# A hybrid decoder block on one core: the recurrence's inverse norm by Newton steps on GpSimd, and pooled tiles loaded into the ring of raw weights

## The chip, the core and the metric

The kernel runs on one core of a Trainium2 chip. The metric is the device time of one execution in microseconds (us). The shapes are fixed: one sequence of 1024 tokens, 1024 channels, 8 heads of 128, four pooling groups of 256 channels, a hidden layer of 4096, everything float32.

The engines are named as in the profile: PE is TensorE's matmul side and PEld its weight load, DVE is VectorE, ACT is ScalarE, POOL is GpSimd, SP is the engine that issues most of the DMAs (SPq is its queue). Each engine takes its instructions in one fixed order.

## What is computed

The reference, cut to what the change touches:

```python
proj = x @ w_in                       # q | f | i | o_gate | pool_v | gate_a | gate_b
o = hgrn2_chunked(...)                # gated recurrence, per head
o = o * rsqrt(mean(o * o) + 1e-6)     # per token and head, over 128 channels
a = (o * hgrn_norm_g * sigmoid(o_gate)) @ w_a
pooled = causal_multiscale_pool(pool_v)           # 4 groups, windows 2, 4, 8, 16
b = concat(pooled[g] @ w_pool[g] for g) * pool_scale
mix = (sigmoid(gate_a) * a + sigmoid(gate_b) * b) @ w_out
x = layer_norm(ALPHA * x + mix)
x = layer_norm(ALPHA * x + relu(x @ w_up) ** 2 @ w_down)
```

## The kernel before, in words

**Products.** Each float32 operand is split into a rounded part and a rest: ACT casts the rounded part (L118), DVE subtracts it from the source to get the rest (L119), and each product is then three matmuls (L105 to L107, or L201, L203, L204). The large projections are 2x2 block products with seven instead of eight block multiplications: `pair` prepares the combinations of weight blocks, `run` walks its seven steps. One step of one pair is 12 matmuls of 128x512.

**Rings.** A weight block arrives as two "raw" tiles from a ring of two buffers (`raw_tile`, 4 KB in each partition), and its split parts lie in a ring of ten "w" tiles (`w_tile`, 2 KB in each partition; `row_tile` is another view of one). A buffer of a ring is handed on when its last reader is done. The recurrence has rings of its own, among them og (2 buffers), v (2), q (3) and f (3), each buffer holding a 128x512 tile.

**The recurrence.** `hgrn(h, u, ...)` works on head h and half u of the tokens, 16 times in all. It decays queries and keys on DVE and POOL (the small chunk factors L819 to L838 are POOL's), transposes keys (L870), forms the state (L875, L883), scores (L887, L898, L905) and outputs in PSUM (L915, L918). Then comes the norm: ACT squares four 128x128 blocks and sums each row (L923), takes the root of the 128x4 sums (L924, which needs another activation table than the sigmoids around it), DVE inverts it (L925), ACT scales the four blocks (L928), PE transposes them (L931), DVE multiplies by the gate (L932), and SP stores the head (L933).

**The order of the work.** The heads are interleaved with the projections: `EXTRAS` lists what follows which half. Behind the last half, (7, 1), stand `gates(4)`, `o_sums(2)`, `pool_products(0)`, `gates(5)`, `pool_products(1)`, `gates(6)`, `pool_products(2)`, `pool_products(3)`, `gates(7)`; the last half itself has a higher priority than these, and so has an `o_sums(3)` inside it, which loads the stored heads 3 and 7 (L594) and adds them up (L608 to L611). The framework records the program and then fixes each engine's order by its own estimate of times; so a small edit can move many instructions. After the heads come `a_pair` (products with w_a), the output product, two layer norms and the hidden layer.

**The pooled products.** `pool_products(g)` loads w_pool of the group into a raw tile (L716) and splits it into q and f buffers. For each half u it loads the two pooled tiles "po" (L594 called from L719) and splits them into w tiles, then does 2 x 6 matmuls (L105 to L107), multiplies by gate and scale (L729, or ACT's L727 for the last group), and stores "pb" (L730). In the kernel before, `room()` hands out q, f, og, v in turn, so the two pooled tiles of a half land in an og and a v buffer of the recurrence's rings.

Of the kernel before, what the change touches and what calls it, by code (L numbers as in the profile page):

```python
# [9 lines left out]
F32 = mybir.dt.float32  # L10
F32R = mybir.dt.float32r
U32 = mybir.dt.uint32
AF = mybir.ActivationFunctionType
ALU = mybir.AluOpType

_TC = dict(schedule_with_timeline_sim=True)
P = 128
# [5 lines left out]
HALF = 512  # L23
CH = HALF // P
# [12 lines left out]
LN_EPS = 1e-5  # L37
RMS_EPS = 1e-6
QSCALE = float(P) ** -0.5
PSUM = bass.MemoryType.PSUM  # L40


@with_exitstack
def tile_hybrid_block(
# [19 lines left out]
    V, A, G, PE = nc.vector, nc.scalar, nc.gpsimd, nc.tensor  # L64
# [5 lines left out]
    const = ctx.enter_context(tc.tile_pool(name="const", bufs=1))  # L70
    pp = ctx.enter_context(tc.tile_pool(name="pp", bufs=4, space=PSUM))
    hd = ctx.enter_context(tc.tile_pool(name="hd", bufs=1, space=bass.MemoryType.DRAM))
# [8 lines left out]
    def nm(s):  # L81
        seq[0] += 1
        return f"{s}_{seq[0]}"
# [7 lines left out]
    def ps_tile(tag="pj", bufs=4):  # L91
        if tag == "hg":
            hg_tags.append(hg_tags.pop(0))
            tag, bufs = hg_tags[-1], 1
        return pp.tile([P, HALF], F32, tag=tag, name=nm("ps_" + tag), bufs=bufs)

    def f(t):
        return t.bitcast(F32)
# [17 lines left out]
    def split(src, tile_of):  # L116
        hi, lo = tile_of(), tile_of()
        A.copy(hi, src)  # L118
        V.tensor_sub(lo, src, f(hi))  # L119
        return hi, lo  # L120
# [11 lines left out]
        out=cmask, in_=cmask, compare_op=ALU.is_ge, fill=0.0, base=0,  # L132
        pattern=[[1, P]], channel_multiplier=-1,
    )
    eps_rms = const.tile([P, 1], F32, name="eps_rms")
    G.memset(eps_rms, RMS_EPS)
    eps_ln = const.tile([P, 1], F32, name="eps_ln")
    G.memset(eps_ln, LN_EPS)
    inv_n = const.tile([P, HALO], F32, name="inv_n")
# [66 lines left out]
    def raw_tile():  # L206
        return wq.tile([P, CH, 2, P], F32, tag="raw", name=nm("raw"), bufs=2)
# [20 lines left out]
    def loaded_blocks(*args):  # L228
        raw, load = w_blocks(*args)
        load(0, 1)  # L230
        return raw
# [28 lines left out]
    def c_late():  # L260
        return c_tile(False)
# [133 lines left out]
    def dram(name, width=HALF):  # L395
        return hd.tile([P, width], F32, tag=name, name=name)
# [5 lines left out]
    with tc.tile_pool(name="xr", bufs=8, side="right", reuse_waits="tile") as xr:  # L402
# [17 lines left out]
        V.tensor_sub(e01[:, 8:16], prm[:, 8:16], lb)  # L420
        A.activation(e01, e01, AF.Exp)
        V.tensor_add(lb, e01[:, 0:8], e01[:, 8:16])
# [157 lines left out]
    pod = [[dram(f"po{j}_{u}") for u in range(2)] for j in range(8)]  # L580
# [11 lines left out]
    def loaded(src, tile_of):  # L592
        t = tile_of()
        nc.sync.dma_start(out=t, in_=src)  # L594
        return t
# [22 lines left out]
    with tc.tile_pool(name="tmp", bufs=1, side="right", reuse_waits="tile") as tmp:  # L618
# [14 lines left out]
        def tt(tag, dtype=F32):  # L633
            pool = tmp if tag in ("q", "f", "og", "v") else hgp
            return pool.tile([P, HALF], dtype, tag=tag, name=nm(tag), bufs=RINGS.get(tag, 1))

        def small(tag, shape, bufs=2):
            n = math.prod(shape[1:])
            t = hgp.tile([P, max(n, LINE)], F32, tag=tag, name=nm(tag), bufs=bufs)[:, :n]
            return t if len(shape) == 2 else t.rearrange("p (a b) -> p a b", b=shape[2])  # L640


        def head_inputs(h, behind=()):
# [6 lines left out]
            def take_f(u):  # L650
                def take(src):
                    t = fs[u] = fs[u] or tt("f")
                    A.activation(t, src, AF.Sigmoid)
                    A.activation(t, t, AF.Identity, bias=lb[:, h : h + 1], scale=one_lb[:, h : h + 1])
                return take

            def take_q(u):
                def take(src):
                    t = qs[u] = tt("q")
                    A.activation(t, src, AF.Sigmoid)  # L660
                    V.scalar_tensor_tensor(t, src, QSCALE, t, ALU.mult, ALU.mult)
                return take
# [11 lines left out]
        def output_gates(h):  # L674

            def take(dst, src=False):
                def put(t):
                    s = c_late() if src else t
                    A.activation(s, t, AF.Sigmoid)
                    nc.sync.dma_start(out=dst, in_=s)  # L680
# [7 lines left out]
        def gates(j):  # L688
# [3 lines left out]
            def take(dst, src=None, more=None):  # L692
                def put(t):
                    s = (tt("v") if spare else c_late()) if src else t
                    more_of = loaded(more, lambda: tt("v")) if more is not None else None
                    A.activation(s, t, AF.Sigmoid)
                    if more_of is not None:
# [10 lines left out]
        def pool_products(g):  # L708

            tags = iter(("q", "f", "og", "v") * 3)  # L710

            def room(dtype=F32):
                return tt(next(tags), dtype)

            raw = raw_tile().rearrange("p k n c -> p (k n c)")[:, : 2 * 2 * P].rearrange("p (k c) -> p k c", c=2 * P)
            nc.sync.dma_start(out=raw, in_=w_pool[g].rearrange("(k p) c -> p k c", p=P))  # L716
            wh, wl = split(raw, lambda: room(F32R).rearrange("p (k c) -> p k c", c=2 * P))
            for u in range(2):
                pl = [split(loaded(pod[2 * g + i][u], room), row_tile) for i in range(2)]  # L719
                for i in range(2):  # L720
                    w = slice(i * P, (i + 1) * P)
                    j = 2 * g + i
                    t = room() if j == KT - 1 else loaded(gbd[j][u], room)
                    ps = ps_tile()
                    mm3(ps, [(wh[:, c, w], wl[:, c, w], *pl[c]) for c in range(2)])
                    if j == KT - 1:
                        A.activation(t, ps, AF.Copy, scale=pscale[:, j : j + 1])  # L727
                    else:
                        V.scalar_tensor_tensor(t, ps, pscale[:, j : j + 1], t, ALU.mult, ALU.mult)  # L729
                    nc.sync.dma_start(out=pbd[j][u], in_=t)  # L730

        def pooled(g):

            j, win = 2 * g, WINDOWS[g]

            def mean(c, u):

                for lo in (QUARTER, 0):
                    pv = c[:, lo : lo + HALO + QUARTER]
                    cur = pv  # L740
                    for lev in range(g + 1):
                        s = 1 << lev
                        nx = small("pA" if lev % 2 == 0 else "pC", [P, HALO + QUARTER + HALO], 1)[:, : HALO + QUARTER]
                        V.tensor_add(nx[:, 2 * s - 1 :], cur[:, 2 * s - 1 :], cur[:, s - 1 : HALO + QUARTER - s])
                        cur = nx
                    n = HALO
                    if u == 0 and lo == 0:
                        n += win - 1
                        V.tensor_mul(cur[:, HALO:n], cur[:, HALO:n], inv_n[:, : win - 1])
                        V.tensor_sub(pv[:, HALO:n], cur[:, HALO:n], pv[:, HALO:n])  # L750
                    V.scalar_tensor_tensor(pv[:, n:], cur[:, n:], 1.0 / win, pv[:, n:], ALU.mult, ALU.subtract)

            def put(c, i, u):
                nc.sync.dma_start(out=pod[j + i][u], in_=c[:, HALO:])

            wide = [[None, None], [None, None]]
            before = small("bef", [P, HALO])

            def room(i, u):
                wide[i][u] = c_wide(False)  # L760
                return wide[i][u][:, HALO:]

            def first(c, i):
                G.memset(c[:, :HALO], 0.0)
                mean(c, 0)
                put(c, i, 0)

            def second(c, i):
                mean(c, 1)
                put(c, i, 1)  # L770

            def take_11(_):
                c = wide[0][0]
                A.copy(before, c[:, HALF:])
                first(c, 0)

            def take_21(_):
                c = wide[0][1]
                A.copy(c[:, :HALO], before)
                second(c, 0)  # L780

            def take_12(ps):
                c, c22 = c_wide(True), wide[1][1]
                A.copy(c[:, HALO:], ps)
                A.copy(c22[:, :HALO], c[:, HALF:])
                first(c, 1)
                second(c22, 1)

            run(pair(
                loaded_blocks(w_in, 4 * D + j * P, 4 * D + (j + 1) * P),  # L790
                (lambda: room(0, 0), lambda: room(0, 1), lambda: room(1, 1)), (take_11, take_12, take_21, lambda _: None),
            ))

        def blk(t):
            return t.rearrange("p (b s) -> p b s", s=SUB)
# [10 lines left out]
        def hgrn(h, u, ft, q, v, og, state):  # L806
# [5 lines left out]
            k = ft  # L812
# [84 lines left out]
            for c in range(CH):  # L897
# [7 lines left out]
            V.copy_predicated(  # L905
                at, cmask.bitcast(U32).unsqueeze(1).to_broadcast([P, CH, P]),
                sc.rearrange("p (c t) -> p c t", t=P),
# [11 lines left out]
            ss = small("ss", [P, CH])  # L919
            on = tt("tH")  # L920
            for c in range(CH):
                w = slice(c * P, (c + 1) * P)
                A.activation(on[:, w], o[:, w], AF.Square, accum_out=ss[:, c : c + 1])  # L923
            A.activation(ss, ss, AF.Sqrt, bias=eps_rms, scale=1.0 / P)  # L924
            V.reciprocal(ss, ss)  # L925
            for c in range(CH):
                w = slice(c * P, (c + 1) * P)
                A.activation(on[:, w], o[:, w], AF.Copy, scale=ss[:, c : c + 1])  # L928
# [153 lines left out]
    with tc.tile_pool(name="wo", bufs=1, side="right", reuse_waits="tile") as mp:  # L1082
        st1 = [None] * 8
        g1, b1 = ln_params(lambda: f(act_tile()).rearrange("p a b -> p (a b)"), ln1_g, ln1_b)
        for k2 in range(0, KT, 2):
            raw = raw_rows(w_out, k2, 1)
            for k in range(2):
                n = len(wo)
# [313 lines left out]
```

## Time and profile before

| What | us |
|---|---|
| time, median of 3 runs | 1464.81 (1462.62 to 1467.08) |
| the profiled execution's own time | 1460.19 |
| its span, first to last instruction | 1458.5 |
| PE busy | 1436.4 |
| DVE busy | 1141.6 |
| ACT busy | 758.3 |
| POOL busy | 58.6 |

The profile is one execution. A group's line gives the source line, the engine, the operation, the tiles it writes and reads, the count, the busy time in us and the mean of one in ns; behind the bar stands the idle time of the engine ahead of such instructions. A view by windows gives for each stretch its length, the busy us of PE, PEld, DVE, ACT and POOL with their instructions in brackets, the granted TensorE clock (1.00 is full), the share of the DMA engines and GB/s. A view of waits gives who waited for whom: us in total, times, the longest. A timeline gives start, length, engine, line and, in brackets, the idle time ahead of an instruction. The list of DMA issues gives the size of one transfer and the median time from issue to landing.

### The profile page before, as it was taken

To read this page: it belongs to the slowest core of one execution; us is meant where nothing else is said; L and a number is where in the kernel's file an instruction comes from. 1 tells how busy PE (TensorE), PEld (TensorE's weight loads), DVE (VectorE), ACT (ScalarE), POOL (GpSimd) and SP (SyncE) were. 2 spreads that over 40 slices of the span, in tenths; PEclk is the share of its full clock that TensorE was granted. 3 is DMA by queue.
4 is the path that set the end of the run, shared out by engine and by line. 5 is a ranking of instruction groups with operands and counts; after the bars stand their busy time and mean duration, and the time that the engine had idled before them with its cause. 6 is when DMAs were issued, how large, how long until landed. Compare 5 with 4: busy or idle time off the path is not lost.

```text
span 1458.5 us, 20662 instructions
## 1 busy us (share of the span) xinstructions
PE 1436.4 (98%) x7377; PEld 1187.9 (81%) x7377; DVE 1141.6 (78%) x1838; ACT 758.3 (52%) x1383; POOL 58.6 (4%) x244
## 2 busy tenths in 40 slices
PE   8999999999999998999999999999999999999997
PEld 7888888888888886788888878888888888888886
DVE  5967989899898885768985597666666787777977
ACT  5445565666656655556542376555555443333535
POOL 0001001001000010000002100000000100000000
PEclk9999999999999999999999999999999999999999
DMA  7232233323234447897672225444474874445322
GB/s 253 70 126 87 85 98 101 109 75 114 90 99 138 152 132 249 301 299 241 223 247 99 73 94 195 159 146 144 152 261 149 275 260 150 153 141 163 130 73 116
DMA packets 160615, 226.82 MB, mean 156 GB/s; under 512 B 11232, under 2 KB 84480, under 8 KB 160512
## 3 DMA queue, kind: packets, MB, share of 16 engines
q1 hardware_dynamic: 158576, 218.93, 44.7%
q0 software_dynamic: 1152, 4.19, 0.8%
q10 hardware_dynamic: 784, 2.38, 0.5%
q8 instruction: 58, 0.95, 0.3%
q14 instruction: 45, 0.37, 0.1%
HBM read 154.16 MB, written 71.30 MB: 155 GB/s over the span
## 4 chain that ended last, share of the span: by engine, by line
PE 94%; DVE 3%; DMA 1%; ACT 1%; issue 0%; SPq 0%; DVEq 0%
PE ps_pj L201 16%; PE ps_pj L203 16%; PE ps_pj L204 16%; PE ps_pj L1283 4%; PE ps_pj L1285 4%; PE ps_pj L1284 4%; PE ps_pj L106 3%; PE ps_pj L107 3%; PE ps_pj L105 2%; PE ps_tr L1285 1%; PE ps_tr L1283 1%; PE ps_tr L1284 1%; PE ps_sc L201 1%; PE ps_sc L203 1%; PE ps_sc L204 1%; PE ps_hg L203 1%
## 5 line engine op out<-in xcount | busy, mean ns | idle before, releaser
L201 PE MATMUL ps_pj<-act,w 128*128 128x512 f32 x1068 | 421.6, 395 | 0.4 <-ACT act L123 0.2
L203 PE MATMUL ps_pj<-act,w 128*128 128x512 f32 x1068 | 415.1, 390 | 0.5 <-DVE act L124 0.5
L204 PE MATMUL ps_pj<-act,w 128*128 128x512 f32 x1068 | 414.1, 390 | 0.0
L201 PEld LDWEIGHTS ps_pj<-act,w 128*128 128x128 f32 x1068 | 200.6, 188 | 42.8 <-ACT act L123 0.6
L204 PEld LDWEIGHTS ps_pj<-act,w 128*128 128x128 f32 x1068 | 200.5, 188 | 42.3
L203 PEld LDWEIGHTS ps_pj<-act,w 128*128 128x128 f32 x1068 | 200.6, 188 | 40.6 <-DVE act L124 0.9
L118 ACT CAST w<-t 128x512 fp32r<-128x512 f32 x170 | 104.7, 620 | 105.0 <-PE ps_pj L203 53.8
L118 ACT CAST w<-raw 128x512 fp32r<-128x512 f32 x143 | 88.2, 620 | 117.3 <-PE ps_pj L203 62.5
L119 DVE TENSOR_TENSOR w<-raw,w 128x512 fp32r<-128x512 f32 x143 | 99.8, 702 | 55.2 <-ACT w L118 53.9
L119 DVE TENSOR_TENSOR w<-t,w 128x512 fp32r<-128x512 f32 x170 | 115.9, 685 | 29.6 <-ACT w L118 29.4
L1245 ACT CAST act<-act 128x1024 fp32r<-128x1024 f32 x66 | 66.9, 1050 | 107.9 <-issue 35.0
L1246 DVE TENSOR_TENSOR act<-act,act 128x1024 fp32r<-128x1024 f32 x66 | 79.3, 1220 | 18.5 <-ACT act L1245 15.8
L1285 PE MATMUL ps_pj<-act,act 128*128 128x512 f32 x240 | 92.9, 389 | 0.0
L1284 PE MATMUL ps_pj<-act,act 128*128 128x512 f32 x240 | 92.9, 389 | 0.0
L1283 PE MATMUL ps_pj<-act,act 128*128 128x512 f32 x240 | 92.4, 389 | 0.0
L275 DVE TENSOR_TENSOR c<-c,ps_pj 128x512 f32<-128x512 f32 x95 | 64.5, 681 | 18.0 <-PE ps_pj L204 13.4
L271 ACT COPY c<-ps_pj 128x512 f32<-128x512 f32 x96 | 55.2, 582 | 12.8 <-PE ps_pj L204 12.8
L817 DVE RECIPROCAL tC<-tA 128x128 f32<-128x128 f32 x64 | 54.1, 904 | 0.0
L1284 PEld LDWEIGHTS ps_pj<-act,act 128*128 128x128 f32 x240 | 45.1, 188 | 9.4
L1285 PEld LDWEIGHTS ps_pj<-act,act 128*128 128x128 f32 x240 | 45.1, 188 | 9.4
L1283 PEld LDWEIGHTS ps_pj<-act,act 128*128 128x128 f32 x240 | 45.1, 188 | 9.3
L241 DVE TENSOR_TENSOR t<-raw,raw 128x512 f32<-128x512 f32 x43 | 29.6, 689 | 21.9 <-DMA raw<-in_w_in_dram 19.7
(415 smaller groups left out, 2719.8 us busy)
## 6 DMA issues: line engine op xcount, KB each, us to landing
h<-c SPq DMA_DIRECT2D x106, 256.0 KB, 2.1
act<-h SPq DMA_DIRECT2D x78, 256.0 KB, 2.9
raw<-in_w_in_dram SPq DMA_DIRECT2D x64, 256.0 KB, 3.4
draw<-in_w_down_dram SPq DMA_DIRECT2D x16, 1024.0 KB, 7.8
raw<-in_w_up_dram SPq DMA_DIRECT2D x30, 512.0 KB, 4.2
raw<-in_w_in_dram SPq DMA_DIRECT2D x18, 512.0 KB, 4.0
hf<-h SPq DMA_DIRECT2D x34, 256.0 KB, 2.9
c<-o SPq DMA_DIRECT2D x24, 256.0 KB, 3.4
```

Source lines behind the costliest of these rows:

```text
L118: A.copy(hi, src)
L119: V.tensor_sub(lo, src, f(hi))
L201: PE.matmul(ps, wh[:, k], th, start=first and k == 0, stop=False, skip_group_check=True)
L203: PE.matmul(ps, wh[:, k], tl, start=False, stop=False, skip_group_check=True)
L204: PE.matmul(ps, wl[:, k], th, start=False, stop=k == CH - 1, skip_group_check=True)
L271: A.copy(t, ps)
L275: V.tensor_add(t, t, ps)
L1245: A.copy(hi, src)
L1246: V.tensor_sub(lo, src, f(hi))
L1283: PE.matmul(ps, hh[:, w], wh, start=fresh and n == 0, stop=False, skip_group_check=True)
L1284: PE.matmul(ps, hh[:, w], wl, start=False, stop=False, skip_group_check=True)
L1285: PE.matmul(ps, hl[:, w], wh, start=False, stop=n == M - 1, skip_group_check=True)
```

## The change

Two edits. First, the root and the reciprocal of the norm (L924, L925) are replaced by `inverse_root`: 14 GpSimd instructions on 128x4 tiles, which take the bits of the number as an integer for a first guess and then make three Newton steps. Its result is a tile "ry", which ACT's scaling (L928) reads instead of "ss". The constant `eps_rms` goes.

Second, the two pooled tiles of a half are loaded into the two halves of one raw tile, `both`, instead of into an og and a v buffer. `room` goes on to hand out q, f, og, v in turn to the other uses of it (the split of w_pool, the loaded gates, the results).

```diff
+ROOT_GUESS = float(0x5F3759DF)
+ROOT_STEPS = 3
...
-    eps_rms = const.tile([P, 1], F32, name="eps_rms")
-    G.memset(eps_rms, RMS_EPS)
...
             for u in range(2):
-                pl = [split(loaded(pod[2 * g + i][u], room), row_tile) for i in range(2)]
+                both = raw_tile().rearrange("p k n c -> p (k n c)").rearrange("p (k c) -> p k c", c=HALF)
+                pl = [split(loaded(pod[2 * g + i][u], lambda: both[:, i]), row_tile) for i in range(2)]
...
+        def inverse_root(total):
+
+            x, y, z = (small(tag, [P, CH]) for tag in ("rx", "ry", "rz"))
+            G.tensor_scalar(x, total, 1.0 / P, RMS_EPS, ALU.mult, ALU.add)
+            G.tensor_scalar(y.bitcast(I32), x.bitcast(I32), -0.5, ROOT_GUESS, ALU.mult, ALU.add)
+            for _ in range(ROOT_STEPS):
+                G.tensor_mul(z, y, y)
+                G.tensor_mul(z, z, x)
+                G.tensor_scalar(z, z, -0.5, 1.5, ALU.mult, ALU.add)
+                G.tensor_mul(y, y, z)
+            return y
...
-            A.activation(ss, ss, AF.Sqrt, bias=eps_rms, scale=1.0 / P)
-            V.reciprocal(ss, ss)
+            ss = inverse_root(ss)
```

Line numbers of the kernel after are higher: by 3 up to the constants, by 1 up to `gates` and `pool_products`, by 13 to 14 from `blk` on. The texts below use the numbers of the kernel before for lines that stand in both.

More of the change, by code (lines that the diff above doesn't have):

```diff
@@ L12 @@
 U32 = mybir.dt.uint32
+I32 = mybir.dt.int32
 AF = mybir.ActivationFunctionType
```

## The prediction, as written before the run

> **What bounds the kernel now.** First the page's head, then the chain that ended last, and the view by windows around the place where the slices of PE dip:
>
> ```profile
> span 1458.5 us, 20662 instructions
> PE 1436.4 (98%) x7377; PEld 1187.9 (81%) x7377; DVE 1141.6 (78%) x1838; ACT 758.3 (52%) x1383; POOL 58.6 (4%) x244
> PE 94%; DVE 3%; DMA 1%; ACT 1%; issue 0%; SPq 0%; DVEq 0%
> ```
>
> ```profile
> 145.00:560.00 415.00, 415.00 (x2763) 345.03 (x2763) 374.35 (x734) 250.82 (x562) 29.35 (x172) 1.00 0.36 113
> 575.00:592.00 17.00, 10.32 (x41) 7.54 (x41) 9.19 (x16) 7.69 (x21) 0.00 (x0) 0.80 0.76 254
> 592.00:640.00 48.00, 48.00 (x212) 39.31 (x211) 31.65 (x51) 22.67 (x39) 0.00 (x0) 1.00 0.95 318
> ```
>
> PE is the bound: 1458.5 - 1436.4 = 22.1 us of idle in all. From 145 to 560 us, which holds almost the whole recurrence, PE has no idle time, so nothing that relieves ACT, DVE or POOL there is worth time. One stretch of 17 us holds 17.00 - 10.32 = 6.7 us of the idle time, and its granted clock of 0.80 costs another 17 x 0.20 = 3.4 us. The view of PE's waits and its timeline tell why:
>
> ```profile
> PE ps_pj L105 <- ACT w L118: 4.7, 1, 4.7
> PE ps_hg L915 <- DVE st L883: 1.2, 1, 1.2
> PE ps_pj L106 <- DVE w L119: 0.8, 1, 0.8
> ```
>
> ```profile
> 572.73 0.39 PE L201 MATMUL ps_pj<-act,w 128*128 128x512 f32 x1
> 572.96 0.39 PE L203 MATMUL ps_pj<-act,w 128*128 128x512 f32 x1
> ...
> 582.85 1.22 PE L105 MATMUL ps_pj<-w,q 128*128 128x512 f32 x2 [4.66 <-ACT w L118]
> ...
> 585.99 0.63 PE L107 MATMUL ps_pj<-w,f 128*128 128x512 f32 x1
> 586.41 0.63 PE L105 MATMUL ps_pj<-w,q 128*128 128x512 f32 x1
> ```
>
> A 128x512 matmul starts 0.23 us after the one before; behind the stall of 4.66 us the step is 0.42 us for a while. The three waits (4.7 + 1.2 + 0.8 = 6.7) are the idle time of that stretch. The chain shows what the longest one waited for:
>
> ```profile
> 573.53 2.31 DMA o<-og
> ...
> 576.27 0.38 SPq L699
> ...
> 577.18 4.97 DMA og<-po
> 582.18 0.62 ACT w L118
> ```
>
> The pooled tile of `pool_products(0)` could be loaded only at 577.18, when the og buffers of the last half came free. **So 6.7 + 3.4 = 10.1 us are to be had in this stretch, and hardly more elsewhere.**
>
> **First edit, the root.** It takes away 16 roots with their table loads, and by the built orders 16 loads that brought the sigmoid's table back (35 loads before, 3 after):
>
> ```profile
> L924 ACT ACT_TABLE_LOAD x16 | 20.5, 1283 | 0.3
> L924 ACT ACTIVATE ss<-ss,eps_rms 128x4 f32<-128x4 f32 x16 | 4.8, 298 | 0.2
> L925 DVE RECIPROCAL ss<-ss 128x4 f32<-128x4 f32 x16 | 2.6, 163 | 5.9 <-ACT ss L924 5.8
> ```
>
> That is 41 us of loads and 4.8 us of roots on ACT, 2.6 us of reciprocals and 5.8 us of waiting on DVE. PE has no idle time where they lie: worth 0.
>
> It adds 14 GpSimd instructions per half, each on the result of the one before. Their nearest rows are small operations of the recurrence:
>
> ```profile
> 401.98 0.22 POOL L823 TENSOR_TENSOR p<-T 128x16 f32<-128x16 f32 x1
> 402.27 0.20 POOL L826 TENSOR_TENSOR p<-p 128x8 f32<-128x8 f32 x1
> ```
>
> ```profile
> L826 POOL TENSOR_TENSOR p<-p x16: 203/204/2201, 127.6 to 537.0; 128x8 f32<-128x8 f32 x16
> L819 POOL COPY T<-tA x16: 229/352/1553, 126.6 to 536.0; 128x32 f32<-128x32 f32 x16
> ```
>
> L826 reads what L823 wrote and starts 0.29 us after it, so 14 x 0.29 = 4.1 us. No row shows GpSimd's multiply-and-add with constants, nor its integer view; from 0.20 us (L826's shortest) to 2.2 us (its longest) each, I take 0.29, the step of the nearest pair. In the chain of a half, 1.28 + 0.30 + 0.16 = 1.7 us become 4.1. What covers them is what stands in PE's order between a half's last L918 and its first transpose L931: in the changed program 47 to 60 large matmuls in fourteen halves and 36 with 23 small ones in another, about 10.7 us or more at 0.23 us, but only 33 (7.5 us) in half (7, 0). Needed are the squares, the root and the first scaling:
>
> ```profile
> L923 ACT ACTIVATE tH<-ps_hg 128x128 f32<-128x128 f32 x64 | 16.9, 279 | 9.1 <-PE ps_hg L918 9.1
> L928 ACT ACTIVATE tH<-ps_hg,ss 128x128 f32<-128x128 f32 x64 | 18.2, 366 | 3.7 <-DVE ss L925 3.7
> ```
>
> The four squares take 4 x 0.28 us, so 1.1 + 4.1 + 0.4 = 5.6 us. In (7, 0) two casts (0.6 us each), one of which needs weights of `gates(5)` that load late, stand on ACT between the squares and the scaling: 0 to 1.5 us of stall, **taken as 0.7**. Without the cover each us more per root would cost up to 16 us.
>
> The first of the 14 instructions waits for ACT's sums. Behind it on POOL stand chunk factors of the next half (L819 to L838), for which DVE's products with T wait. About six DVE instructions at 0.6 to 0.9 us stand between the scan and the first of these, against 0.3 us for each root instruction put in between: taken as 0.
>
> **Second edit, the raw ring.** The two pooled tiles are loaded into a raw buffer. In the changed orders `pool_products(0)` stands before the last half's outputs and 24 large matmuls stand between L875 and L915: all three waits of 575 to 592 go, **-10.1 us**. What is late next? The raw ring has only two buffers, X and Y, and now carries a chain: w_pool[g] in X, then the first half's pooled tiles in X, the second half's in Y, then the next `gates` in X and Y. No link can be loaded before the last is split. The prices, from the list of DMA issues between 540 and 640 us and from the groups:
>
> ```profile
> raw<-in_w_in_dram SPq DMA_DIRECT2D x10, 256.0 KB, 5.6
> og<-po SPq DMA_DIRECT2D x8, 256.0 KB, 3.9
> raw<-in_w_pool_dram SPq DMA_DIRECT2D x4, 256.0 KB, 4.1
> tC<-o SPq DMA_DIRECT2D x1, 256.0 KB, 3.7
> ...
> L118 ACT CAST w<-raw 128x512 fp32r<-128x512 f32 x143 | 88.2, 620 | 117.3 <-PE ps_pj L203 62.5 <-DMA raw<-in_w_in_dram 16.7 <-PE ps_sc L203 10.2
> L932 DVE SCALAR_TENSOR_TENSOR og<-ps_tr,prm,og 128x512 f32<-128x512 f32 x16 | 11.9, 745 | 0.2 <-PE ps_tr L931 0.2
> ```
>
> ```profile
> 590.24 0.68 DVE L119 TENSOR_TENSOR w<-og,w 128x512 fp32r<-128x512 f32 x1
> 590.84 0.68 DVE L119 TENSOR_TENSOR w<-v,w 128x512 fp32r<-128x512 f32 x1
> ```
>
> DVE steps of this size start 0.6 us apart. For groups 0 and 1 the links are covered by 8 and 5 us of matmuls. For **group 2** they meet the end of the recurrence. On SP, the load of w_pool[2] stands right behind the load tC of the last head, which waits for that head's store; on DVE, its split stands behind the sums that need tC. From the gated product L932: store 2.3 us (the chain's row), tC 3.7 with 0.4 us of issue on SP, four DVE steps at 0.6 (two sums, a split, w_pool's split) 2.4, load of po 3.9, cast 0.6, and issues 0.2: 13.5 us. L932 itself is late, since a difference of `gates(6)`'s weights stands three places ahead of it on DVE. The last of these weights is issued when a w buffer has come free (23 matmuls, 5.2 us, ahead of the transposes) and a cast and a split (1.4 us with the issue) have used it, and lands 5.6 + 0.4 us later, 2.2 us behind the first transpose; four DVE steps (2.5 us) later L932 is done, at 4.7. PE has its four transposes (0.5 us) and 61 large matmuls (13.9) in between: 4.7 + 13.5 - 14.4 = **3.8 us of stall**. With the shortest loads of these kinds in this stretch (2.9 and 2.6 us) it vanishes; with the longest (8.5 and 7.9) it is 10:
>
> ```profile
> DMA to landing us min/median/max: 2.9/5.3/8.5
> ...
> DMA to landing us min/median/max: 2.7/3.9/7.9
> ...
> DMA to landing us min/median/max: 2.6/3.6/7.2
> ```
>
> (These are the views by tile of raw, og and v.) For **`gates(7)`**, X comes free only with the split of group 3's first tiles, and ACT's order puts the scaling of the last pooled product, which waits for the product's end, ahead of the first cast: at least 0.2 + 0.6 + 0.6 = 1.4 us of stall, and with a load of 5.6 us, issued 4 us before that end, 2.2; **taken as 2.0**, up to 5. Group 3's own load, behind three 512 KB loads of w_a, adds 0.2.
>
> A new stall may also lower the clock. 4.66 us did so and cost 3.4 us, 1.2 us did not; 3.8 lies between, nearer the first, but PE's full pace had been cut by three waits there: 1 in 4, 0.8 us. [...]
>
> **Sum:** -10.1 + 0.7 + 3.8 + 2.0 + 0.2 + 0.8 = -2.6 us against the profiled execution's 1460.19 (its span and 1.7 us around it): 1457.6. The runs shown have a median of 1464.81, 4.6 us above it, so I expect 1462.2, say **1462**.
>
> **Rivals.** (1) *Clean gain.* The loads land near their short end, since the stretch from 577 on no longer bunches them: group 2's stall goes, `gates(7)` keeps 1.4, half (7, 0) 0.5: -8.2 us, 1456.6. For it: PE waits nowhere from 592 to 640 in spite of 318 GB/s. Against it: the ring's links are in sequence. (2) *Late links, slower.* The loads of the chain land at 8 us, behind the 1.5 MB of w_a: stalls of 10 and 4.5 us, with the clock halved after both (6.8) and 0.7 more: 22 - 10.1 = +11.9, 1476.7. It is slower as soon as the new stalls and their slow clock cost over 10.1 us. (3) *The root outgrows its cover, slower.* It decides where the root takes over 10.7 - 1.5 = 9.2 us, 0.66 us for an instruction; at 1.0 us it is 14, and 15 halves stall by 4.8 us, +72, 1537. L819's median of 0.35 and the longest of 2.2 us speak for it, L826's median of 0.20 against it. [...] (4) *The change does nothing:* the tiles are loaded no earlier and the stall stays, 1464.8; the new order of SP speaks against it.
>
> **Chances.** A run can hardly tell less than 0.3% (4.4 us) from no change. Forecast, with most of the gain given back, and rival 4: 0.43, within 0.3%. Rival 1: 0.40, faster. Rivals 2 and 3: 0.11 and 0.06, slower. The range: down to 1453 (all 10.1 us, less 2 us of spread as in the runs shown), up to 1470, where rival 2 has half its price; beyond lie about 0.15. The forecast's own range is 1458 to 1469.
>
> **What would show it.** Right: no wait of L105 for group 0; a wait of PE at the first matmul of group 2, ended by ACT's cast of a raw tile, and one at the first of `gates(7)`; 3 table loads on ACT; root steps of about 0.3 us; PE without idle time in the recurrence. Wrong: PE waits for L931 in many halves (the root is too slow), or no wait at groups 2 and 3 at all (rival 1).

## The result, and the profile after

| What | us |
|---|---|
| time of the changed kernel, median of 4 runs | 1488.41 (1487.62 to 1491.49) |
| time of the kernel before beside it, median of 4 runs | 1464.82 (1462.62 to 1467.08) |
| ratio | 1.0165, 95% interval 1.0144 to 1.0186 |
| the profiled execution's own time, and its span | 1488.09, 1486.4 |

The change makes the kernel 23.6 us slower. The forecast was 1462, its range ended at 1470, and no rival named what happened. The head of the profile's page of the changed kernel, and its chain by engines:

```profile
span 1486.4 us, 20806 instructions
PE 1463.7 (98%) x7377; PEld 1192.3 (80%) x7377; DVE 1142.7 (77%) x1822; ACT 715.2 (48%) x1335; POOL 120.4 (8%) x467
PE 91%; DVE 4%; DMA 3%; issue 1%; ACT 1%; SPq 0%; DVEq 0%; ACTq 0%
```

PE has the same 7377 matmuls, and its idle time is 1486.4 - 1463.7 = 22.7 us, against 22.1 before. So the span did not grow by waits. PE's *busy* time grew, by 1463.7 - 1436.4 = 27.3 us: the matmuls themselves take longer. The view by lines, kept apart by shape, tells which. The kernel before (after the bar's first number, the busy time, stands the mean of one in ns):

```profile
L201 PE MATMUL ps_pj<-act,w 128*128 128x512 f32 x1068 | 421.6, 395 | 0.4 <-ACT act L123 0.2 <-ACT og L271 0.2
L203 PE MATMUL ps_pj<-act,w 128*128 128x512 f32 x1068 | 415.1, 390 | 0.5 <-DVE act L124 0.5
L204 PE MATMUL ps_pj<-act,w 128*128 128x512 f32 x1068 | 414.1, 390 | 0.0
L1285 PE MATMUL ps_pj<-act,act 128*128 128x512 f32 x240 | 92.9, 389 | 0.0
```

The changed kernel, the same products:

```profile
L202 PE MATMUL ps_pj<-act,w 128*128 128x512 f32 x1068 | 427.6, 401 | 3.6 <-ACT w L121 2.4 <-ACT room L272 0.6 <-DVE v L731 0.4
L204 PE MATMUL ps_pj<-act,w 128*128 128x512 f32 x1068 | 421.5, 396 | 0.5 <-DVE act L127 0.5
L205 PE MATMUL ps_pj<-act,w 128*128 128x512 f32 x1068 | 421.0, 397 | 0.6 <-DVE w L122 0.6
L1297 PE MATMUL ps_pj<-act,act 128*128 128x512 f32 x240 | 93.0, 390 | 0.0
```

Every product of an `act` tile with a `w` tile takes 6 to 7 ns more; a product of two `act` tiles takes what it took. The three lines alone add 6.0 + 6.4 + 6.9 = 19.3 us. The view by windows shows the same as a pace, far from both edits. From 900 to 1150 us PE does nothing but products of act with w (the recurrence and the pooled products are long over), from 1200 to 1400 only products of act with act. Before:

```profile
900.00:1150.00 250.00, 250.00 (x1105) 207.07 (x1104) 162.85 (x239) 142.13 (x236) 2.32 (x4) 1.00 0.51 174
1200.00:1400.00 200.00, 200.00 (x884) 165.62 (x883) 158.83 (x173) 74.82 (x77) 0.00 (x0) 1.00 0.44 145
```

After:

```profile
900.00:1150.00 250.00, 250.00 (x1073) 201.79 (x1072) 156.00 (x237) 137.22 (x233) 0.00 (x0) 1.00 0.48 167
1200.00:1400.00 200.00, 200.00 (x884) 165.67 (x883) 158.89 (x173) 76.41 (x79) 0.00 (x0) 1.00 0.50 164
```

PE is busy all the time at a granted clock of 1.00 in both, so neither a wait nor the throttle is at work. But 1105 matmuls became 1073: 250 / 1105 = 226 ns each became 250 / 1073 = 233. Behind 1200 us nothing changed. A share "98% busy" cannot show this; the count of instructions in a window does.

What the prediction said of the second edit can be read in PE's waits of the changed kernel:

```profile
PE ps_pj L108 <- ACT w L121: 4.2, 1, 4.2
PE ps_pj L202 <- ACT w L121: 2.4, 2, 2.1
```

Group 0 waits no longer; the wait at L108 is the first matmul of group 2, the longest one at L202 the first of `gates(7)`. What they did to the clock stands in the windows around them (the clock is the third number from the end):

```profile
634.00:640.00 6.00, 4.38 (x12) 3.49 (x13) 1.99 (x3) 3.14 (x6) 0.00 (x0) 0.72 0.86 294
...
655.00:660.00 5.00, 2.87 (x12) 1.78 (x11) 1.44 (x2) 1.62 (x3) 0.00 (x0) 0.95 1.05 343
660.00:668.00 8.00, 8.00 (x29) 6.37 (x29) 6.84 (x12) 5.57 (x10) 0.00 (x0) 0.82 0.83 268
```

Both stalls were followed by a slow stretch, each worth 1.7 us (6 x 0.28; 5 x 0.05 + 8 x 0.18).

### The profile page after: what moved, and what is told of

It reads as the page before. It is cut to its first block, busy times and chain, and to the rows that moved or that the text cites. A ratio compares the mean times of both kernels' runs of the same rounds, so it can differ in the third digit from the quotient of the medians.

```text
span 1486.4 us, 20806 instructions
## 1 busy us (share of the span) xinstructions
PE 1463.7 (98%) x7377; PEld 1192.3 (80%) x7377; DVE 1142.7 (77%) x1822; ACT 715.2 (48%) x1335; POOL 120.4 (8%) x467
## 4 chain that ended last, share of the span: by engine, by line
PE 91%; DVE 4%; DMA 3%; issue 1%; ACT 1%; SPq 0%; DVEq 0%; ACTq 0%
PE ps_pj L202 16%; PE ps_pj L205 16%; PE ps_pj L204 16%; PE ps_pj L1298 4%; PE ps_pj L1297 4%; PE ps_pj L1296 4%; PE ps_pj L108 2%; PE ps_pj L110 2%; PE ps_pj L109 2%; PE ps_tr L1298 1%; PE ps_tr L1297 1%; PE ps_tr L1296 1%; PE ps_sc L202 1%; PE ps_sc L204 1%; DMA raw<-in_w_in_dram 1%; PE ps_sc L205 1%
## 5 line engine op out<-in xcount | busy, mean ns | idle before, releaser
L202 PE MATMUL ps_pj<-act,w 128*128 128x512 f32 x1068 | 427.6, 401 | 3.6 <-ACT w L121 2.4
L204 PE MATMUL ps_pj<-act,w 128*128 128x512 f32 x1068 | 421.5, 396 | 0.5 <-DVE act L127 0.5
L205 PE MATMUL ps_pj<-act,w 128*128 128x512 f32 x1068 | 421.0, 397 | 0.6 <-DVE w L122 0.6
L202 PEld LDWEIGHTS ps_pj<-act,w 128*128 128x128 f32 x1068 | 201.6, 189 | 52.1 <-ACT w L121 3.3
L122 DVE TENSOR_TENSOR w<-raw,w 128x512 fp32r<-128x512 f32 x159 | 111.0, 703 | 77.3 <-ACT w L121 76.0
L121 ACT CAST w<-raw 128x512 fp32r<-128x512 f32 x159 | 98.3, 621 | 146.1 <-PE ps_pj L204 81.2
```

The costliest lines, as they stand in the source:

```text
L202: PE.matmul(ps, wh[:, k], th, start=first and k == 0, stop=False, skip_group_check=True)
L204: PE.matmul(ps, wh[:, k], tl, start=False, stop=False, skip_group_check=True)
L205: PE.matmul(ps, wl[:, k], th, start=False, stop=k == CH - 1, skip_group_check=True)
```

## The experiments

Theories. **A, place:** with `eps_rms` the first edit takes away not only a constant but its slot. In the built programs a [128, 1] constant takes 32 bytes per partition, and what is allocated behind it on the same side moves by 32 bytes, the whole ring `act` among it. The tiles `w` are allocated from the other side and stay. The theory: the pace of a matmul depends on how the addresses of its two operands lie to each other. **B, root:** GpSimd's new work slows PE. **C, ring:** the pooled tiles in the raw ring slow it. Against B stands the view by tile of the changed kernel's first root instruction (shortest, median and longest in ns, first and last start in us):

```profile
L799 POOL TENSOR_SCALAR rx<-ss x16: 190/194/612, 166.6 to 608.6; 128x4 f32<-128x4 f32 x16
```

The last root starts at 608.6, and the slow pace stands from 900 to 1150 us. But that is reading, not a test.

**The changed kernel with the old place, in two ways.** First an unused constant in the place of eps_rms:

```diff
+    spare_col = const.tile([P, 1], F32, name="spare_col")
+    G.memset(spare_col, RMS_EPS)
```

> The changed kernel with an unused 4-byte constant where eps_rms stood, so that the tiles allocated behind it (the ring act among them) have the addresses of the kernel before; both edits stay. Theory A (place: act lies 32 bytes off, and some 4020 products of an act tile with a w tile cost 6.4 ns more each, 26 us in all): 1461 to 1464 us, the median spacing of the products of act and w back from 233 to 227 ns. Theory B (the root's steps on GpSimd slow TensorE): 1488, 233 ns. Theory C (the pooled tiles in the raw ring slow it): 1488, 233 ns.

Measured: 1467.86 us, ratio to before 1.0037 (1.0024 to 1.0050). The second way moves w by as much as act had moved and leaves every engine's instructions and their order alone:

```diff
-    G.memset(pad.tile([P, 24], F32, name="pad_top"), 0.0)
+    G.memset(pad.tile([P, 32], F32, name="pad_top"), 0.0)
```

> The changed kernel with one edit: pad_top 32 bytes longer, so that w moves down by as much as the missing eps_rms had moved act, and their distance is what it was before the change; no constant is added and every engine has the same instructions in the same order as in the changed kernel. Theory A: 1467 to 1469 us (the changed kernel's 1488 less some 20 to 24), spacing of the products of act and w 227 ns. Theories B and C: 1488, 233 ns.

Measured: 1466.68 us, ratio 1.0020 (1.0011 to 1.0029), just under what was expected. Its row of the same window:

```profile
900.00:1150.00 250.00, 250.00 (x1105) 207.08 (x1104) 162.24 (x241) 144.04 (x239) 0.31 (x1) 1.00 0.50 171
```

1105 matmuls again, with both edits in place. Of the change's 1.65% this takes back 1.45%, **21 us**; theories B and C are out as causes of the pace. In the first way 1461 to 1464 us were expected: the pace is back, but some 5 us stay, so the edits cost something of their own.

**The kernel before, moved.** The unused constant in the kernel before (act moves, neither edit is there):

> The kernel before with one more unused 4-byte constant, so that act and what is allocated behind it move by 32 bytes; neither edit is in it. Theory A: 1489 to 1492 us, spacing of the products of act and w 233 ns, the products of act with act still 227. Theories B and C: 1465, 227 ns.

Measured: 1483.38 us, 1.0142 (1.0127 to 1.0158). The longer pad_top alone (w moves, act stays):

> The kernel before with pad_top 32 bytes longer and no unused constant: w and the other tiles on its side are 32 off, act is where it was. Relative form of theory A: 1489 to 1492 us, spacing of the products of act and w 233 ns. Absolute form, if it is act alone that counts: 1465. Absolute form, if any operand off counts: 1490. Theories B and C: 1465.

Measured: 1482.40 us, 1.0135 (1.0118 to 1.0152). So moving either operand by 32 bytes costs about 20 us of a kernel that is otherwise the same; it is not act that must lie well. (The 26 us of the theory were too much. With the unused constant the busy time of the three lines of products above grows by 16.6 us, and 3.0 more in the six groups of 80 for the other tiles in PSUM; the profiled executions differ by 1483.92 - 1460.19 = 23.7, the medians by 20.4, since the profiled execution of before is among its fastest.) The window with the longer pad_top:

```profile
900.00:1150.00 250.00, 250.00 (x1073) 200.85 (x1072) 157.00 (x239) 137.89 (x233) 0.00 (x0) 1.00 0.48 166
```

Now both, by the constant and the longer pad_top:

> The kernel before with the unused constant and with pad_top 32 bytes longer, so that act and w both move by 32 bytes: each is 32 off a multiple of 64, and they agree with each other. Theory A in its relative form (the two operands of a product must have the same phase): 1464 to 1466 us, spacing 227 ns. Theory A in its absolute form (an operand off a multiple of 64 costs): 1490 or more, spacing 233 or more. Theories B and C: 1465.

Measured: 1473.75 us, 1.0075 (1.0060 to 1.0090), between the forms of the theory. The two sides grow towards each other, so these two edits move act up and w down: their distance had changed by 64 bytes, not by 0 as the expectation's wording has it. Two kernels set that right. Both up by 32, with the constant and a shorter pad_top ([P, 16]):

> The kernel before with an unused 4-byte constant (act 32 bytes up) and with pad_top 32 bytes shorter (w 32 bytes up too), so that act and w keep the distance that they had, and both are 32 off a multiple of 64. In the kernel with pad_top longer their distance had changed by 64 bytes, and the products of act with w took 229 to 231 ns. If only the distance between the two operands counts (theory A, relative): 1463 us, spacing 227 ns. If the place of each by itself counts: 1474 or more, 229 ns or more.

Measured: 1464.31 us, 1.0005 (0.9996 to 1.0015). And act alone up by 64, with two unused constants:

> The kernel before with two unused 4-byte constants: act 64 bytes up, w where it was. If the distance counts modulo 64: 1463 us, 227 ns. If it counts modulo 128: as in the kernel where act and w moved by 32 bytes in opposite directions, 1473 to 1475 us, 229 to 231 ns. If only an operand off a multiple of 64 counts: 1463.

Measured: 1472.39 us, 1.0068 (1.0054 to 1.0081). The runs in one table (addresses within a partition, modulo 128 bytes, as the programs place them; matmuls from 900 to 1150 us by the view by windows):

| kernel | act, w | distance | matmuls | ratio |
|---|---|---|---|---|
| before | 0, 0 | 0 | 1105 | 1 |
| before, both up by 32 | 32, 32 | 0 | 1105 | 1.0005 |
| changed, w moved | 96, 96 | 0 | 1105 | 1.0020 |
| changed, unused constant | 0, 0 | 0 | 1104 | 1.0037 |
| before, two constants | 64, 0 | 64 | 1094 | 1.0068 |
| before, act up, w down | 32, 96 | 64 | 1094 | 1.0075 |
| before, longer pad_top | 0, 96 | 32 | 1073 | 1.0135 |
| before, one constant | 32, 0 | 32 | 1073 | 1.0142 |
| changed | 96, 0 | 96 | 1073 | 1.0165 |

The distance of the two operands modulo 128 sorts the pace without an exception: 226 ns at 0, 250 / 1094 = 229 at 64, 233 at 32 and 96. The place of either by itself does nothing. That the period is 128 is not shown: the table holds the distance of the kernel before and shifts by 32 and 64 bytes from it, so a longer period, 256 or 512, would sort these runs as well. In the programs the distances at the fast pace are multiples of 512; no run moved the operands by 128 against each other.

**The root alone**, with the unused constant:

```diff
-                both = raw_tile().rearrange("p k n c -> p (k n c)").rearrange("p (k c) -> p k c", c=HALF)
-                pl = [split(loaded(pod[2 * g + i][u], lambda: both[:, i]), row_tile) for i in range(2)]
+                pl = [split(loaded(pod[2 * g + i][u], room), row_tile) for i in range(2)]
```

> The first edit alone (root by Newton steps), with an unused 4-byte constant where eps_rms stood, so that act keeps its address. Prediction's account of the edit (hidden but for 0.7 us in one half): ratio to before 1.000 to 1.001, 1463 to 1464 us. Theory B in what is left of it (the root's steps come late in the first halves, where act's second changed copy shows waits of 0.86 and 0.79 us at 140.5 and 136.9 us): 1.001 to 1.002. If the root also disturbs more than these halves: over 1.003.

Measured: 1466.90 us, 1.0034 (1.0021 to 1.0047): not hidden, about 5 us. PE's waits and, of half (7, 0), PE's timeline in that kernel:

```profile
PE ps_tr L945 <- ACT tH L942: 3.4, 1, 3.4
PE ps_hg L930 <- DVE st L898: 2.6, 2, 1.4
PE ps_pj L108 <- ACT w L121: 1.8, 1, 1.8
```

```profile
574.76 0.39 PE L206 MATMUL ps_pj<-act,w 128*128 128x512 f32 x1
574.99 0.39 PE L207 MATMUL ps_pj<-act,w 128*128 128x512 f32 x1
578.80 0.48 PE L945 MATMUL ps_tr<-ident,tH 128*128 128x128 f32 x1 [3.42 <-ACT tH L942]
```

The transposes of (7, 0) wait for the scaling behind the root. The price lies at this end of the recurrence: from 540 to 600 us PE idles for 8.8 us at a clock of 0.89, against 6.75 us at 0.94 in the kernel before. In this kernel's order only 12 large matmuls stand between that half's outputs and its transposes; in the kernel before there are 24. Was it the root in this half, then? The root in heads 0 to 6 only:

```diff
-            ss = inverse_root(ss)
+            if h == HEADS - 1:
+                A.activation(ss, ss, AF.Sqrt, bias=eps_rms, scale=1.0 / P)
+                V.reciprocal(ss, ss)
+            else:
+                ss = inverse_root(ss)
```

> The kernel before with the root on GpSimd in heads 0 to 6 and the old root in head 7; the pooled tiles as before, act at its old address. In the kernel with the root alone PE waited 3.4 us in half (7, 0) for the scaling behind the root. If the root costs only there: 1463 us, ratio 1.000 to 1.001, with 1 us left in the first halves at most. If it costs in the whole recurrence: 1466, as with the root in all halves (1.0034).

Measured: 1465.92 us, 1.0020 (1.0011 to 1.0028): the ratio lies between the two that were expected, and the interval excludes both. Head 7 has its old root back, and PE still waits in it:

```profile
PE ps_hg L930 <- DVE st L898: 4.2, 2, 2.2
...
PE ps_hg L890 <- ACT tH L887: 1.9, 1, 1.9
...
PE ps_tr L949 <- ACT tH L946: 0.7, 1, 0.7
```

PE's order is the new one: the first scores of (7, 0) start 11 us later than in the kernel before (here the row of before, then that of this kernel), and 12 large matmuls instead of 24 stand inside that half.

```profile
549.97 0.46 PE L887 MATMUL sc<-tF,tD 128*32 128x32 f32 x32
```

```profile
560.94 0.46 PE L902 MATMUL sc<-tF,tD 128*32 128x32 f32 x32
```

By this reading a part of the root's price comes not from a late root but from the order that the framework makes of the changed program: the end of the recurrence has less to stand beside it. No run changed the order alone.

**The ring alone**, on the kernel before:

```diff
-                pl = [split(loaded(pod[2 * g + i][u], room), row_tile) for i in range(2)]
+                both = raw_tile().rearrange("p k n c -> p (k n c)").rearrange("p (k c) -> p k c", c=HALF)
+                pl = [split(loaded(pod[2 * g + i][u], lambda: both[:, i]), row_tile) for i in range(2)]
```

> The second edit alone (pooled tiles for w_pool's products in the raw ring); eps_rms stays, so act keeps its address. The prediction's account: -2.6 us, ratio 0.998. Account from the windows of the changed kernel with act at its old address (550 to 600 us: -8.0; 600 to 650: +9.1; 650 to 700: +3.6; sum +4.7): ratio 1.003, 1467 to 1468 us.

Measured: 1464.28 us, 1.0009 (0.9998 to 1.0020). Is it the ring's chain at groups 2 and 3 that eats the gain? `both` only where g < 2, the others through `room` as before:

```diff
+                both = raw_tile().rearrange("p k n c -> p (k n c)").rearrange("p (k c) -> p k c", c=HALF) if g < 2 else None
+                pl = [split(loaded(pod[2 * g + i][u], room if both is None else lambda: both[:, i]), row_tile) for i in range(2)]
```

> The kernel before with the raw ring for the pooled tiles of groups 0 and 1 only; groups 2 and 3 load theirs into the og and v buffers as before; no root edit, act at its old address. With all four groups in the ring 550 to 600 us lost 6.6 us (before: 11.1), but 600 to 700 lost 9.2 (before: 0.8). If the ring's chain from group 2 on is what gives the gain back: 600 to 700 us as before, sum -4 us, 1458 to 1460. If the loss moves with the first groups: 1463 to 1465.

Measured: 1465.09 us, 1.0019 (1.0008 to 1.0030). And with g < 1 in the place of g < 2:

> As the last, for group 0 only, the one whose load came late in the kernel before. If the prediction's 10.1 us are to be had there: 1453 to 1456. If other links of the last half are late as soon as that wait goes: -2 to -5 us, 1458 to 1461. If the ring costs as much as it gives: 1463.

Measured: 1464.04 us, 1.0004 (0.9995 to 1.0013). The gain is there, and given back later, even where groups 1 to 3 are loaded as before. The two stretches in the kernel before:

```profile
540.00:600.00 60.00, 53.25 (x300) 42.83 (x299) 38.76 (x71) 29.95 (x70) 0.00 (x0) 0.94 0.69 228
600.00:720.00 120.00, 119.85 (x527) 98.30 (x526) 95.87 (x155) 68.66 (x121) 0.00 (x0) 1.00 0.83 275
```

and with the ring for group 0 alone:

```profile
540.00:600.00 60.00, 58.38 (x333) 47.47 (x332) 41.07 (x75) 33.63 (x77) 0.00 (x0) 1.00 0.73 242
600.00:720.00 120.00, 112.16 (x483) 89.27 (x482) 91.20 (x146) 61.97 (x109) 0.00 (x0) 1.00 0.78 264
```

Up to 600 us PE's idle time falls from 6.75 to 1.62 us and the slow clock (60 x 0.06 = 3.6 us) goes: 8.7 us won. From 600 to 720 the idle time grows from 0.15 to 7.84: 7.7 us lost. What is left, 1.0 us, doesn't show in the medians. The chain of the kernel with the ring for group 0 says where:

```profile
620.15 6.64 DMA q<-gb
626.85 7.28 DMA og<-po
634.22 0.62 ACT w L118
635.78 0.62 ACT w L118
```

In the kernel before the chain of this stretch is PE's matmuls one behind the other. Here it leaves PE at 618.9 us and runs over transfers of 6.6 and 7.3 us, later over others. Two of the loads on which the last products depend start almost when they started before. SP's timeline in the kernel before:

```profile
627.29 0.70 SPq L594 DMA_DIRECT2D og<-po  x1
...
640.49 0.94 SPq L223 DMA_DIRECT2D raw<-in_w_in_dram  x2
```

and with the ring for group 0:

```profile
626.85 0.94 SPq L594 DMA_DIRECT2D og<-po  x1
...
639.76 1.30 SPq L223 DMA_DIRECT2D raw<-in_w_in_dram  x2
```

PE comes 8.7 us earlier, the first of the last four pooled tiles 0.4 us, the last of them 3.5 (issued at 632.07 instead of 635.58 us), and the weights of `gates(7)` 0.7. The transfers also took longer, and the DMA engines were fuller. From 620 to 640 us (the share of the DMA engines is the number before the last), in the kernel before and with the ring for group 0:

```profile
620.00:640.00 20.00, 20.00 (x90) 16.56 (x89) 10.37 (x17) 9.56 (x17) 0.00 (x0) 1.00 0.90 296
```

```profile
620.00:640.00 20.00, 18.55 (x80) 14.39 (x79) 11.95 (x19) 9.33 (x17) 0.00 (x0) 1.00 1.03 359
```

The two pooled tiles loaded into og buffers there took a median of 4.9 us from issue to landing before, and 7.1 now. So a chain of transfers stood close behind PE, and 8.7 - 7.7 = 1.0 us is all that came through. This is read from chain, timeline and windows; no kernel was run that makes those transfers faster or starts them earlier, and how much of the 7.7 us is late starts and how much full DMA engines stays open. No version that was run beats the kernel before.

## Why the prediction was wrong

**Failed: the sum itself had no term for where tiles lie.** The step is the account of the first edit: table loads, roots and reciprocals go, "worth 0", and 14 GpSimd instructions come. `eps_rms` was listed in the change as gone and got no price. Its 32 bytes are the result: 21 of 23.6 us by the kernel with w moved. With it failed the premise that a 128x512 matmul "starts 0.23 us after the one before" whatever the change does; the prediction priced waits and clock, and the pace was taken as given. In the runs the pace is 226, 229 or 233 ns, sorted by the distance of a product's two operands, at a granted clock of 1.00 and without a wait. What in the chip sets it, no run shows.

**Right: the bound, and the table loads' worth.** PE is the bound, and has no idle time in the recurrence of the changed kernel:

```profile
150.00:560.00 410.00, 410.00 (x2651) 336.20 (x2650) 359.68 (x692) 203.83 (x502) 84.22 (x367) 1.00 0.35 109
```

ACT's table loads are gone but for three, and PE's windows show nothing gained.

**Mis-sized but harmless: 14 x 0.29 = 4.1 us for a root.** From 408 us, in the changed kernel (first, fourth, fifth and last of the 14):

```profile
408.27 0.19 POOL L799 TENSOR_SCALAR rx<-ss 128x4 f32<-128x4 f32 x1 [17.86 <-ACT tH L937]
...
409.10 0.65 POOL L803 TENSOR_TENSOR rz<-rz,rx 128x4 f32<-128x4 f32 x1
409.83 0.51 POOL L804 TENSOR_SCALAR rz<-rz 128x4 f32<-128x4 f32 x1
...
414.11 0.32 POOL L805 TENSOR_TENSOR ry<-ry,rz 128x4 f32<-128x4 f32 x1
```

That root takes 414.43 - 408.27 = 6.2 us (the 16 of them take 4.2 to 7.5), and DVE is busy beside it:

```profile
408.20:414.40 6.20, 6.20 (x28) 4.98 (x27) 5.34 (x12) 1.94 (x3) 5.06 (x15) 1.00 0.27 89
```

DVE works 5.34 of 6.20 us. In the kernel with the root alone there is a root beside a DVE that idles until 577.60 us (its first two instructions and its last, and the window):

```profile
573.96 0.19 POOL L800 TENSOR_SCALAR rx<-ss 128x4 f32<-128x4 f32 x1 [23.56 <-ACT tH L938]
574.24 0.20 POOL L801 TENSOR_SCALAR ry<-rx 128x4 int32<-128x4 int32 x1
...
577.61 0.74 POOL L806 TENSOR_TENSOR ry<-ry,rz 128x4 f32<-128x4 f32 x1
```

```profile
573.90:578.40 4.50, 1.48 (x7) 0.90 (x5) 0.77 (x2) 0.62 (x2) 3.31 (x14) 0.89 0.76 286
```

A step is 0.28 us, and the 14 take 578.35 - 573.96 = 4.4; only the last, of 0.74 us, runs beside a DVE instruction. So one instruction took 0.19 to 0.20 us beside an idle DVE, and 0.24 to 0.65 from the fourth on in the root of the changed kernel, beside a busy one. What lengthens them, no run shows. Rival 3 needed 0.66 us for each; here it is 6.2 / 14 = 0.44, and the cover held: PE waits for no scaling behind a root in the changed kernel.

**Half right: half (7, 0), 0.7 us.** 0 in the changed kernel, 1.5 in the same program with w moved, 3.4 in the one with the root alone. The price hangs on an order that each further edit changes, and on the pace that the place sets.

**Right: the ring's new stalls.** Group 2 was forecast at 3.8 us and measured at 4.2, `gates(7)` at 2.0 and 2.1. Group 0's wait is gone. That the figure for group 2 is so close is in part luck: the gated product (L932, now L945) ended 2.9 us behind the first transpose instead of 4.7, and the links from there to the first matmul took 16.0 us instead of 13.5.

**Mis-sized: the clock, 0.8 us.** It is 3.4 (twice 1.7), since it fell behind both stalls: to 0.72 from 634 to 640 us, with the stall of 4.2 us, and to 0.82 from 660 to 668 us, behind the one of 2.1. In the kernel before it had been 0.50 from 582.8 to 588 us, behind 4.66 us. The prediction's 0.8 us was its estimate for the stall of group 2 alone. The length of a stall does not decide alone. The longest waits of two other kernels, with the ring for group 0 and for groups 0 and 1, were longer than 2.1 us:

```profile
PE ps_pj L201 <- ACT w L118: 2.4, 1, 2.4
```

```profile
PE ps_pj L201 <- ACT w L118: 3.0, 2, 2.8
```

Behind both the clock stayed at 1.00 (in each 20 us from 600 to 720). What decides, the runs do not show.

**Failed: "10.1 us are to be had in this stretch".** Up to 600 us 8.7 were won with the ring for group 0 alone, but a chain of transfers stood right behind PE and took 7.7 back. The forecast of -2.6 us, -3.3 without the 0.7 of the root, became with the ring alone +1.3 (1.0009, by its interval -0.3 to +2.9). The prediction looked for what is late next only along the raw ring, and did not ask how much slack the other transfers of 600 to 720 us had once PE comes 9 us earlier.

Together: place 21 us, the two edits 2.9 (1.0020, with 1.6 to 4.2 by its interval), by the kernel with w moved; by the one with the unused constant the two edits cost some 5 (1.0037). Alone they cost 5.0 and 1.3, so they may overlap, but the two kernels do not settle it. In the profiled executions part of what the edits cost was hidden in the changed kernel: with w moved PE idles for 1465.6 - 1438.6 = 27.0 us instead of 22.7, since at the faster pace it comes earlier to what it waits for.

## What to carry to other kernels

When busy time grows at the same count of instructions and full clock, count instructions per window and compare the pace group by group before looking for a wait. An edit that adds or drops a constant moves every tile behind it (here by 32 bytes, worth about 20 us): before crediting the edit, run it with the old addresses kept by an unused tile of the same size, and when tiles of two pools are multiplied, keep the distance that had the fast pace (226 ns a matmul here, against 229 and 233; no run tells whether another multiple of 128 bytes would do as well). And a stall that is taken away is worth only the slack of the chain behind it (here 1.0 of 8.7 us): look up how close the transfers of the next 100 us run to the bound, and how full the DMA engines are there.

## What the runs showed of the hardware that was not expected

- A 128x512 matmul of an act tile with a w tile starts every 226 ns at the distance that their addresses have in the kernel before, every 229 ns with that distance changed by 64 bytes, every 233 ns with it changed by 32 either way, all at a granted clock of 1.00; only the distance counts (both moved by 32: 1105 matmuls in 250 us, as with neither moved).
- A stretch of slow clock, at 0.82, followed a stall of PE of 2.1 us (1.7 us lost, as much as with one of 4.2 us, at 0.72); behind stalls of 2.4 and 2.8 us in two other kernels the clock stayed at 1.00.
- Small GpSimd instructions that follow each other take 0.28 us a step with DVE idle and 0.44 on average with DVE at 5.34 of 6.20 us.
